# Two blocks on one core: a modelled DMA queue in the order planner, four key projections side by side, and the last three gate projections in token halves

## The chip, the cores and the metric

One core of one Trainium2 chip runs the whole program as one launch. The metric is the device time of that core in microseconds; lower is better. 2911.86 us is the median of three runs of the kernel before (2909.01 to 2912.65).

## The reference, cut to what matters

512 tokens of width 2048 go through two residual blocks. What follows is the frame that the change touches: the memory projections at the start, and the gate and the final norm at the end.

```python
def memory_cross_attention(xq, mem_n, w_kv, qn_g, kn_g):       # first block
    q = rms_norm(xq.reshape(B, S, XA_HEADS, XA_DIM), qn_g)
    kv = jnp.einsum("bmd,de->bme", mem_n, w_kv)                # 256 memory rows
    k = rms_norm(kv[..., :XA_WIDTH]..., kn_g); v = kv[..., XA_WIDTH:]...
    p = jax.nn.softmax(q . k * XA_DIM ** -0.5)
    return p . v

def first_block(x, mem, ...):
    mem_n = rms_norm(mem, mem_norm_g)
    h = rms_norm(x, norm_g)
    proj = jnp.einsum("bsd,de->bse", h, dn_w_in)
    mix = deltanet_branch(proj[..., :DN_MIX_COLS], ...)        # conv, gated delta rule
    xa = memory_cross_attention(xq, mem_n, ...)
    y = jnp.concatenate([mix, xa], axis=-1) * jax.nn.silu(z)
    return x + jnp.einsum("bse,ed->bsd", y, w_out)

def second_block(x, p, ...):
    ...                                                        # mLSTM and HGRN2 mixers
    h = h + jnp.einsum('bsc,cd->bsd', y, w_out)
    e = jnp.einsum('bsr,rd->bsd', p, w_pe)
    gate = jax.nn.sigmoid(jnp.einsum('bsd,de->bse', rmsnorm(h, pe_norm_w), w_pg))
    h = h + gate * e
    return rmsnorm(h, final_norm_w)
```

## The kernel before, in words

Activations lie feature-major: a tile is 128 features by 512 tokens (256 for the memory), and 2048 features are 16 such tiles. Every large product is done in float32 by a split: ScalarE rounds an operand to `hi` (L120), VectorE makes the rest `lo` (L131), and TensorE adds hi times hi, hi times lo and lo times hi into one PSUM bank (L167). A weight job is 128 output features; its weights come in four pieces of 4 feature tiles, 128 by 512 numbers or 256 KB each. A piece goes through a `raw` buffer (six of them), a `hi` buffer and a `lo` buffer (five each), and feeds 12 products on TensorE: for each of the four feature tiles hi times the high and the low half of the activation, then lo times the high half.

The program is written by a planner in Python, `Driver` (from L80). It keeps an estimated clock for each engine (`clk`), and a generator for every piece of work. `run` (L348) takes the ready task of the best priority, or else the next three products, and issues its instructions on the engines' queues at once. So the clocks only set the order; the chip runs each engine's queue strictly in that order, and every instruction waits for what it needs. Loads stand on SyncE's queue in order too. In the planner of before a weight piece was held to be there at 3 us behind TensorE's clock, or at 4.5 us plus 1.5 us for each piece, whichever is later (L274), and any other load after 2.3 us (L171).

The stages that matter here:

- **Start.** SyncE loads a piece of `w_k` and a tile pair of the memory (`mraw`, L450) in turn, eight times, and then a piece and a tile of x (`xraw`, L456) in turn, sixteen times. Of the 16 jobs of the memory (8 keys, 8 values, 256 columns in every product) the first two stand side by side: a pair of feature tiles feeds both before the next is needed (L1739, `add`). `mem_task` (L560) scales and splits the memory (`mh`, `ml`) and then sums its squares (`mraw`); `evac_k` and `evac_v` wait for the sum. `x_task` (L591) squares x on ScalarE (`xsq`), sums on VectorE (`xsum`), gets the reciprocal norm over TensorE (`ss`), and then `part` scales each of the 16 tiles of x and splits it (`xraw`, `xh`, `xl`).
- **Query projections.** The first jobs on x (`acc<-xh`) use these 16 tiles one by one.
- **Middle.** The first block's convolutions and delta rule, output, the second block's mixers, and its output.
- **End.** Jobs `je[i]` and `jg[i]` alternate (16 of each). `evac_g` (L1689) scales the gate's product, takes the sigmoid, multiplies by `e`, adds to `h` and adds the square to a sum. The last gate job is done in two halves of 256 tokens. At the end of each half comes the sum over features (`ss`), the reciprocal root (ScalarE Ln and Exp), and 16 products of 128 by 256 (`out`), 13 of them on VectorE and 3 on GpSimd, which leave as 8 stores of 256 KB.

## Time and profile before

| what | value |
|---|---|
| median of three runs | 2911.86 us (2909.01 to 2912.65) |
| the profiled execution, its own time | 2909.73 us |
| its span in the trace | 2907.8 us |
| TensorE busy | 2852.8 us, 98% |
| VectorE busy | 1713.4 us, 59% |
| ScalarE busy | 1389.0 us, 48% |
| GpSimd busy | 80.7 us, 3% |
| DMA | 308.92 MB, mean 106 GB/s |

TensorE is busy nearly all the time, so a look at shares tells little; what is left to gain lies where TensorE waits. Matmul durations overlap in the trace: the distance between two starts is what a product costs. "Idle before, releaser" names what ended a wait.

### The profile page before, as it was taken

What the parts mean: (1) busy time and instruction counts of PE and PEld (TensorE: products, weight loads), DVE (VectorE), ACT (ScalarE), POOL (GpSimd) and SP (SyncE); (2) the same over time, 40 slices, a digit from 0 to 9 for tenths busy, and PEclk for the clock granted to TensorE, in tenths of its full rate; (3) what the DMA queues carried; (4) which work ended last, traced back from release to release, by engine and by line L of the source; (5) the groups of instructions that cost most, each with busy time, mean ns of one, the idle gap of its engine ahead of it and who ended that gap; (6) DMA issues with size and microseconds to landing.
All of it is one profiled execution on the core that took longest, in us unless ns stands there. A gap on an engine that the chain in (4) does not pass through costs nothing. (4 is left out here: it accounts for less than half of the span.)

```text
span 2907.8 us, 40891 instructions
## 1 busy us (share of the span) xinstructions
PE 2852.8 (98%) x14936; PEld 2382.5 (82%) x14936; DVE 1713.4 (59%) x3285; ACT 1389.0 (48%) x2627; POOL 80.7 (3%) x178
## 2 busy tenths in 40 slices
PE   7999999999999999999999999999999999999997
PEld 7877887788788888888888878888888888888886
DVE  6746677778777777635333464455655556444445
ACT  6544645565545555435222334444554556433433
POOL 0000000100000100000000000000000000000000
PEclk9999999999999999999999999999999999999998
DMA  7422422233222332354433433222222222333233
GB/s 244 145 80 93 122 94 88 95 98 98 83 89 98 95 98 91 102 169 127 130 119 119 151 104 109 91 77 80 84 84 77 91 84 88 116 122 110 95 98 109
DMA packets 177865, 308.92 MB, mean 106 GB/s; under 512 B 25216, under 2 KB 32000, under 8 KB 177664
## 3 DMA queue, kind: packets, MB, share of 16 engines
q1 hardware_dynamic: 177664, 306.31, 33.1%
q8 instruction: 117, 1.92, 0.3%
q14 instruction: 84, 0.69, 0.1%
HBM read 290.24 MB, written 15.99 MB: 105 GB/s over the span
## 5 line engine op out<-in xcount | busy, mean ns | idle before, releaser
L131 DVE TENSOR_TENSOR lo<-raw,hi 128x512 fp32r<-128x512 f32 x948 | 638.5, 685 | 624.4 <-ACT hi L120 605.5
L120 ACT ACTIVATE hi<-raw 128x512 fp32r<-128x512 f32 x956 | 586.9, 621 | 868.6 <-PE acc L167 762.4
L167 PE MATMUL acc<-xh,hi 128*128 128x512 f32 x1424 | 582.5, 409 | 0.7 <-ACT xh L120 0.4
L167 PE MATMUL acc<-xl,hi 128*128 128x512 f32 x1424 | 556.2, 391 | 2.8 <-DVE xl L131 2.7
L167 PE MATMUL acc<-xh,lo 128*128 128x512 f32 x1408 | 551.4, 392 | 4.5 <-DVE lo L131 4.4
L167 PE MATMUL acc<-x2h,hi 128*128 128x512 f32 x1040 | 415.8, 400 | 0.0
L167 PE MATMUL acc<-x2l,hi 128*128 128x512 f32 x1040 | 405.2, 390 | 0.0
L167 PE MATMUL acc<-x2h,lo 128*128 128x512 f32 x1024 | 399.8, 390 | 0.0
L167 PEld LDWEIGHTS acc<-xh,lo 128*128 128x128 f32 x1408 | 264.4, 188 | 63.8 <-DVE lo L131 6.2
L167 PEld LDWEIGHTS acc<-xl,hi 128*128 128x128 f32 x1424 | 268.4, 189 | 54.6 <-DVE xl L131 4.0
L167 PEld LDWEIGHTS acc<-xh,hi 128*128 128x128 f32 x1424 | 268.2, 188 | 53.6 <-issue 1.7
L167 PE MATMUL acc<-ph,hi 128*128 128x512 f32 x768 | 298.8, 389 | 0.0
L167 PE MATMUL acc<-pl,hi 128*128 128x512 f32 x768 | 298.8, 389 | 0.0
L167 PE MATMUL acc<-ph,lo 128*128 128x512 f32 x768 | 298.8, 389 | 0.0
L167 PEld LDWEIGHTS acc<-x2h,lo 128*128 128x128 f32 x1024 | 192.2, 188 | 41.5
L167 PEld LDWEIGHTS acc<-x2l,hi 128*128 128x128 f32 x1040 | 195.7, 188 | 37.0
L167 PEld LDWEIGHTS acc<-x2h,hi 128*128 128x128 f32 x1040 | 195.6, 188 | 37.2
L167 PEld LDWEIGHTS acc<-pl,hi 128*128 128x128 f32 x768 | 144.1, 188 | 30.1
L167 PEld LDWEIGHTS acc<-ph,lo 128*128 128x128 f32 x768 | 144.1, 188 | 29.9
L167 PEld LDWEIGHTS acc<-ph,hi 128*128 128x128 f32 x768 | 144.1, 188 | 29.8
L134 DVE SCALAR_TENSOR_TENSOR cv<-acc,c_dn_conv,cv 128x511 f32<-128x511 f32 x144 | 107.3, 747 | 35.6 <-ACT cv L120 32.1
L131 DVE TENSOR_TENSOR Xb<-Xb,Nb 128x16 f32<-128x16 f32 (+30 forms) x372 | 113.7, 306 | 8.8
(321 smaller groups left out, 3631.4 us busy)
## 6 DMA issues: line engine op xcount, KB each, us to landing
raw<-w_qkv SPq DMA_DIRECT2D x192, 256.0 KB, 3.1
raw<-w_out SPq DMA_DIRECT2D x192, 256.0 KB, 2.9
raw<-w_z SPq DMA_DIRECT2D x128, 256.0 KB, 3.2
raw<-w_pg SPq DMA_DIRECT2D x68, 256.0 KB, 3.0
gR<-dgc SPq DMA_DIRECT2D x48, 256.0 KB, 3.9
raw<-w_k SPq DMA_DIRECT2D x32, 256.0 KB, 4.8
raw<-w_v SPq DMA_DIRECT2D x32, 256.0 KB, 3.7
raw<-w_xq SPq DMA_DIRECT2D x32, 256.0 KB, 3.1
```

Source lines behind the costliest of these rows:

```text
L120: self.nc.scalar.activation(out=out, in_=in_, func=func, **kw)
L131: self._v(eng, free_size(out)).tensor_tensor(out=out, in0=a, in1=b, op=op)
L134: self._v(None, free_size(out)).scalar_tensor_tensor(out=out, in0=a, scalar=s, in1=b, op0=op0, op1=op1)
L167: self.nc.tensor.matmul(out, lhsT=lhsT, rhs=rhs, start=start, stop=stop, is_transpose=True if tr else None)
```

## The change

The planner gets a clock for SyncE and one for the DMA queue (`land`, in place of the fixed delays): a load starts when SyncE can issue it, the queue then takes 1.1 us for 256 KB at first and 0.7 us later, and the load is held to be there a little after. Weight pieces, the first loads and all later loads and stores through `dma` use it. Since every clock steers the order, instructions move in the whole program, though the same work is done.

At the start the first four key jobs stand side by side instead of two; the eight tile pairs of the memory are loaded over the first 13 pieces of weights, with six tiles of x between them, and the other ten tiles of x after 16 pieces. The squares of x are summed on GpSimd instead of VectorE.

At the end the last three gate jobs instead of one are done in token halves, all three of the first half ahead of the second half's. Their squares move from ScalarE to VectorE. The 16 output products of a half are a task of their own (`out_half`); four of the 16 are on GpSimd.

```diff
 
     def __init__(self, tc, wp, psp, sp):
         self.tc, self.nc, self.wp, self.psp, self.sp = tc, tc.nc, wp, psp, sp
-        self.clk = dict(pe=0.0, act=0.0, dve=0.0, pool=0.0)
+        self.clk = dict(pe=0.0, act=0.0, dve=0.0, pool=0.0, sp=1.2)
+        self.dq = 0.0
         self.tau = 0.0
         self.tasks = []
         self.units = []
@@ -168,9 +169,17 @@
                               is_transpose=True if tr else None)
         self._on("pe", c, LP)
 
-    def dma(self, out, in_, lat=2.3):
+    def land(self, n=128 * T, extra=0.1):
+
+        t = max(self.clk["pe"], self.clk["sp"])
+        self.clk["sp"] = t + 0.5
+        self.dq = max(self.dq, t + 2.0)
+        self.dq += (0.7 if self.dq > 9 else 1.1) * n / (128 * T)
+        return self.dq + 0.25 + extra
+
+    def dma(self, out, in_, extra=0.9, n=128 * T):
         self.nc.sync.dma_start(out=out, in_=in_)
-        self.tau = max(self.tau, self.clk["pe"]) + lat
+        self.tau = max(self.tau, self.land(n, extra))
 
 
     def slot(self, shape=(128, T), dt=F32, name="s", reserve=0):
@@ -271,7 +280,7 @@
             j, c0, n = self.pieces[self.i_dma]
             raw = self.wp.tile([128, KC, 128], F32, tag="raw", bufs=RAW, name="raw")
             self.nc.sync.dma_start(out=raw[:, :n, :j.w.shape[2]], in_=j.w[:, c0:c0 + n])
-            self.pieces[self.i_dma] = (j, c0, n, raw, max(self.clk["pe"] + 3.0, 4.5 + 1.5 * self.i_dma))
+            self.pieces[self.i_dma] = (j, c0, n, raw, self.land(n * 128 * j.w.shape[2]))
             self.i_dma += 1
             if self.i_dma <= self.nhead:
                 self.head(self.i_dma)
...
@@ -444,19 +453,31 @@
     for k in range(KT):
         xraw.append(d.slot_now(name="xraw"))
 
+    loads = [[] for _ in range(1 + 3 * KT)]
+    for i in range(len(mraw)):
+        loads[4 * (i // 2) + (i % 2 if i < 2 else i % 2 - 1)].append(("m", i))
+    n = 0
+    for i in range(len(loads)):
+        if n < KT and (i % 4 in (1, 2) and i > 4 if i < KT else i >= KT):
+            loads[i].append(("x", n))
+            n += 1
+
     def first_loads(i):
 
-        if i < len(mraw):
-            nc.sync.dma_start(out=mraw[i], in_=A["memT"][:, 2 * i:2 * i + 2])
-        elif i < len(mraw) + KT:
-            k = i - len(mraw)
+        for what, k in loads[i] if i < len(loads) else ():
+            if what == "m":
+                nc.sync.dma_start(out=mraw[k], in_=A["memT"][:, 2 * k:2 * k + 2])
+                f_m[k].tau = d.land()
+                f_m[k].done = True
+                continue
             if k == 0:
                 nc.sync.dma_start(out=ident, in_=A["ident"])
                 nc.sync.dma_start(out=norm_g, in_=A["norm_g"])
             nc.sync.dma_start(out=xraw[k], in_=A["xT"][:, k])
-            d.give(f_x[k])
-            f_x[k].tau = d.clk["pe"] + 3.0
-
+            f_x[k].tau = d.land(extra=0.5)
+            f_x[k].done = True
+
+    f_m = [Fut() for _ in mraw]
     f_x = [Fut() for _ in range(KT)]
     resetb = const.tile([128, T], F32, name="resetb")
     nc.vector.memset(resetb, 1.0)
...
@@ -560,7 +581,8 @@
     def mem_task():
         hs = []
         for i, t in enumerate(mraw):
-            d.tau = 3.8 + 1.5 * i
+            d.tau = 0.0
+            yield from need(f_m[i])
             yield
             tau = d.tau
             hi = yield from slot(dt=F32R, name="mh")
@@ -577,6 +599,7 @@
         t0 = d.tau
         for i, t in enumerate(mraw):
             d.tau = t0
+            yield from need(f_m[i])
             yield from d.calm(AHEAD)
             t = t.rearrange("p k m -> p (k m)")
             act(t, t, AF.Square)
@@ -592,13 +615,14 @@
         ssum = yield from slot(name="xsum")
         for k, t in enumerate(xraw):
             yield from need(f_x[k])
+            yield
             yield from d.calm(AHEAD)
             q = yield from slot(name="xsq")
             act(q, t, AF.Square)
             if k == 0:
-                cp(ssum, q)
+                cp(ssum, q, eng=pool)
             else:
-                tt(ssum, ssum, q, ADD)
+                tt(ssum, ssum, q, ADD, eng=pool)
             free(q)
         f = Fut()
         yield from ones_sum([ssum], T, 1.0 / D, f)
...
@@ -1686,13 +1710,18 @@
             give(f_pe[i], e)
         return gen
 
+    NSP = 3
+
+    def on_pool(k):
+        return k % 3 == 1 and k < KT - NSP
+
     def evac_g(i):
         def gen(job):
             r = yield from need(f_r2)
             w = cst("fin_w")
             c, n = job.cols, job.n
-            t = yield from slot(name="gt")
-            t = t[:, :n]
+            job.t = yield from slot(name="gt")
+            t = job.t[:, :n]
             tt(t, job.ps, r[:, c], MUL)
             d.acc_done()
             act(t, t, AF.Sigmoid)
@@ -1702,44 +1731,60 @@
             tt(t, t, e[:, c], MUL)
             h = f_h2[i].val[:, c]
             tt(h, h, t, ADD)
-            if i < KT - 1:
-                free(t, e)
+            if c.stop == T:
+                free(e)
+            if i < KT - NSP:
+                free(job.t)
                 yield from sum_sq("h3", h, i == 0)
-                if i % 4 == 3:
+                if on_pool(i):
                     act(h, h, AF.Copy, scale=w[:, i:i + 1])
                 return
-            act(t, h, AF.Square)
+            tt(t, h, h, MUL)
+            if i < KT - 1:
+                tt(ssq["h3"][:, c], ssq["h3"][:, c], t, ADD)
+                free(job.t)
+                return
             yield
             ss = yield from bank("ss")
             mm(ss[:, :n], ones, ssq["h3"][:, c], start=True, stop=False)
             mm(ss[:, :n], ones, t, start=False, stop=True)
             rstd(ss[:, :n], t, 1.0 / D)
             d.free_bank()
-            t0 = d.tau
-            for k0 in range(0, KT, 2):
+            last = c.stop == T
+            d.spawn(out_half(c, n, t, last), 4 if last else 30)
+        return gen
+
+    def out_half(c, n, t, last):
+
+        w = cst("fin_w")
+        t0 = d.tau
+        for k0 in range(0, KT, 2):
+            o = yield from slot((128, 2, n), name="out")
+            te = []
+            for k in (k0, k0 + 1):
                 d.tau = t0
-                o = yield from slot((128, 2, n), name="out")
-                for k in (k0, k0 + 1):
-                    d.tau = t0
-                    yield
-                    h = f_h2[k].val[:, c]
-                    if k % 4 == 3 and k < KT - 1:
-                        tt(o[:, k - k0], h, t, MUL, eng=pool)
-                    else:
-                        stt(o[:, k - k0], h, w[:, k:k + 1], t, MUL, MUL)
-                nc.sync.dma_start(out=out[:, k0:k0 + 2, c], in_=o)
-        return gen
+                if not last:
+                    yield from d.calm(AHEAD)
+                h = f_h2[k].val[:, c]
+                if on_pool(k):
+                    tt(o[:, k - k0], h, t, MUL, eng=pool)
+                else:
+                    stt(o[:, k - k0], h, w[:, k:k + 1], t, MUL, MUL)
+                te.append(d.tau)
+            d.tau = max(te)
+            yield
+            nc.sync.dma_start(out=out[:, k0:k0 + 2, c], in_=o)
 
 
     first_loads(0)
     d.head = first_loads
-    d.nhead = len(mraw) + KT
+    d.nhead = len(loads) - 1
...
     d.spawn(mem_task(), 1)
     d.spawn(x_task(), 2)
     jk = [Job(A["w_k"][e], M, evac_k(e), NM) for e in range(2 * XH)]
     jv = [Job(A["w_v"][e], M, evac_v(e), NM) for e in range(2 * XH)]
-    d.add(jk[0], jk[1])
-    for j in jk[2:] + jv[:-2]:
+    d.add(*jk[:4])
+    for j in jk[4:] + jv[:-2]:
         d.add(j)
     jv[-1].drop = True
     d.add(jv[-2], jv[-1])
@@ -1857,12 +1902,14 @@
     d.add(je[0])
     d.add(je[1])
     d.add(jg[0], jg[1])
-    for i in range(2, KT - 1):
+    for i in range(2, KT - NSP):
         d.add(je[i])
         d.add(jg[i])
-    d.add(je[KT - 1])
-    d.add(Job(A["w_pg"][KT - 1], X3, evac_g(KT - 1), n=T // 2))
-    d.add(Job(A["w_pg"][KT - 1], X3, evac_g(KT - 1), n=T // 2, prio=4, c0=T // 2))
+    for i in range(KT - NSP, KT):
+        d.add(je[i])
+    for c0 in (0, T // 2):
+        for i in range(KT - NSP, KT):
+            d.add(Job(A["w_pg"][i], X3, evac_g(i), n=T // 2, c0=c0, prio=4))
     with tc.manual_schedule():
         d.run()
```

Left out of the diff are the calls of `dma` in the gates' and mixers' tasks, which now give the size of what they load.

Three places in the queues, before and after. The first is ScalarE's queue at the start (`hi<-raw`: a weight piece's high half; `mh`: the memory's; `xsq`: squares of x; `mraw`: squares of the memory). Before:

```order
L120 ACTIVATE hi<-raw 128x512
L120 ACTIVATE mh<-mraw,c_mem_norm_g 128x256 x2
L120 ACTIVATE hi<-raw 128x512
L120 ACTIVATE mh<-mraw,c_mem_norm_g 128x256 x2
L120 ACTIVATE xsq<-xraw 128x512
L120 ACTIVATE hi<-raw 128x512
L120 ACTIVATE mh<-mraw,c_mem_norm_g 128x256 x2
L120 ACTIVATE hi<-raw 128x512
L120 ACTIVATE xsq<-xraw 128x512
```

After:

```order
L121 ACTIVATE hi<-raw 128x512
L121 ACTIVATE mh<-mraw,c_mem_norm_g 128x256 x2
L121 ACTIVATE hi<-raw 128x512
L121 ACTIVATE xsq<-xraw 128x512
L121 ACTIVATE hi<-raw 128x512 x2
L121 ACTIVATE mh<-mraw,c_mem_norm_g 128x256 x2
L121 ACTIVATE xsq<-xraw 128x512
L121 ACTIVATE hi<-raw 128x512
L121 ACTIVATE mh<-mraw,c_mem_norm_g 128x256 x2
```

Both begin with the fourth weight piece, and in both the first square of x stands behind the fifth. On SyncE's queue, which is not shown, the first tile of x is loaded behind the eighth weight piece before and behind the fifth after.

The second place is VectorE's queue where x is scaled and split, from the row in which the sum of squares goes to TensorE (`ql<-xsum`) or near it (`lo<-raw`: a weight piece's low half; `vt`: a value job's result; `xraw<-xraw`: scaling a tile of x; `xl`: its low half). Before, the last part of that stretch:

```order
L131 TENSOR_TENSOR xl<-xraw,xh 128x512
L131 TENSOR_TENSOR lo<-raw,hi 128x512
L131 TENSOR_TENSOR xl<-xraw,xh 128x512
L134 SCALAR_TENSOR_TENSOR xraw<-xraw,norm_g,xsum 128x512 x3
L131 TENSOR_TENSOR lo<-raw,hi 128x512
L134 SCALAR_TENSOR_TENSOR xraw<-xraw,norm_g,xsum 128x512 x2
L131 TENSOR_TENSOR xl<-xraw,xh 128x512 x3
L134 SCALAR_TENSOR_TENSOR xraw<-xraw,norm_g,xsum 128x512
L131 TENSOR_TENSOR xl<-xraw,xh 128x512 x2
L134 SCALAR_TENSOR_TENSOR xraw<-xraw,norm_g,xsum 128x512
L131 TENSOR_TENSOR lo<-raw,hi 128x512
L131 TENSOR_TENSOR xl<-xraw,xh 128x512 x2
```

After, the same part:

```order
L132 TENSOR_TENSOR lo<-raw,hi 128x512
L135 SCALAR_TENSOR_TENSOR xraw<-xraw,norm_g,xsum 128x512 x4
L132 TENSOR_TENSOR xl<-xraw,xh 128x512
L135 SCALAR_TENSOR_TENSOR xraw<-xraw,norm_g,xsum 128x512
L132 TENSOR_TENSOR xl<-xraw,xh 128x512 x5
L135 SCALAR_TENSOR_TENSOR xraw<-xraw,norm_g,xsum 128x512 x2
L132 TENSOR_TENSOR lo<-raw,hi 128x512
L135 SCALAR_TENSOR_TENSOR xraw<-xraw,norm_g,xsum 128x512 x3
L132 TENSOR_TENSOR xl<-xraw,xh 128x512 x2
L135 SCALAR_TENSOR_TENSOR xraw<-xraw,norm_g,xsum 128x512
L132 TENSOR_TENSOR xl<-xraw,xh 128x512 x3
L132 TENSOR_TENSOR lo<-raw,hi 128x512
```

The `lo` of the 70th weight piece stands in front of the block of after; the first row is that piece. Behind it 11 scalings and 12 low halves are left (one low half follows the last row). Before, behind the 70th piece's `lo`, which is the row between the first two `xl`, 7 scalings and 8 low halves are left. On TensorE's queue the sum of squares (`ss`) stands behind 600 of the 768 products of the memory before, and behind 684 of them after.

The third place is the end of VectorE's queue (`gt`, `h1r`, `ssum`: the evacuation of a gate job). Before:

```order
L131 TENSOR_TENSOR lo<-raw,hi 128x512 x4
L131 TENSOR_TENSOR gt<-acc,ssum 128x256
L131 TENSOR_TENSOR gt<-gt,e 128x256
L131 TENSOR_TENSOR h1r<-h1r,gt 128x256
L131 TENSOR_TENSOR gt<-acc,ssum 128x256
L131 TENSOR_TENSOR gt<-gt,e 128x256
L131 TENSOR_TENSOR h1r<-h1r,gt 128x256
L134 SCALAR_TENSOR_TENSOR out<-h1r,c_fin_w,gt 128x256 x26
```

After, from the evacuation of the last job but one:

```order
L132 TENSOR_TENSOR gt<-acc,ssum 128x256
L132 TENSOR_TENSOR gt<-gt,e 128x256
L132 TENSOR_TENSOR h1r<-h1r,gt 128x256
L132 TENSOR_TENSOR gt<-h1r 128x256
L132 TENSOR_TENSOR ssum<-ssum,gt 128x256
L132 TENSOR_TENSOR lo<-raw,hi 128x512 x3
L135 SCALAR_TENSOR_TENSOR out<-h1r,c_fin_w,gt 128x256 x10
L132 TENSOR_TENSOR gt<-acc,ssum 128x256
L132 TENSOR_TENSOR gt<-gt,e 128x256
L132 TENSOR_TENSOR h1r<-h1r,gt 128x256
L132 TENSOR_TENSOR gt<-h1r 128x256
L135 SCALAR_TENSOR_TENSOR out<-h1r,c_fin_w,gt 128x256 x14
```

Ten output products of the first half now stand ahead of the last job's evacuation, and three `lo` of the last job's own weights stand behind the evacuation of the job before it.

## Rows read from the trace of the kernel before

**Rows 1.** The page: TensorE's busy time, share of the span, instructions.

```profile
PE 2852.8 (98%) x14936; PEld 2382.5 (82%) x14936; DVE 1713.4 (59%) x3285; ACT 1389.0 (48%) x2627; POOL 80.7 (3%) x178
```

**Rows 2.** Busy time by stretch (us from the span's start: length, then busy time and instructions of each engine, granted clock of TensorE, DMA share, GB/s).

```profile
0.00:72.70 72.70, 58.02 (x437) 56.30 (x438) 49.61 (x98) 48.69 (x97) 0.20 (x4) 0.98 0.76 244
...
10.00:20.00 10.00, 6.62 (x49) 6.28 (x48) 5.75 (x13) 5.83 (x13) 0.00 (x0) 1.00 0.97 313
...
2880.00:2907.80 27.80, 8.10 (x59) 7.19 (x58) 16.94 (x35) 7.59 (x14) 5.33 (x6) 0.72 0.45 151
```

**Rows 3.** What TensorE waited for, over the whole span (us in total, times, longest).

```profile
PE acc L167 <- DVE lo L131: 9.2, 6, 3.2
...
PE pst L167 <- DVE ud L131: 3.2, 1, 3.2
PE tr L167 <- DVE pr L131: 3.0, 4, 1.3
...
PE p L167 <- DVE XA L141: 2.5, 2, 1.3
PE num L167 <- DVE Cs L134: 2.1, 1, 2.1
```

**Rows 4.** The same from the start to 135 us.

```profile
PE acc L167 <- ACT mh L120: 6.3, 1, 6.3
PE acc L167 <- DVE lo L131: 4.7, 3, 2.7
PE acc L167 <- ACT hi L120: 3.4, 1, 3.4
PE acc L167 <- DVE xl L131: 2.7, 2, 1.8
```

**Rows 5.** ScalarE in order of time, 13 to 20 us (start, duration, instruction, idle time before it and its releaser).

```profile
13.30 0.61 ACT L120 ACTIVATE hi<-raw 128x512 fp32r<-128x512 f32 x1
13.82 0.90 ACT L120 ACTIVATE mh<-mraw,c_mem_norm_g 128x256 fp32r<-128x256 f32 x2
18.39 0.63 ACT L120 ACTIVATE xsq<-xraw 128x512 f32<-128x512 f32 x1 [3.68 <-DMA xraw<-xT]
18.93 0.61 ACT L120 ACTIVATE hi<-raw 128x512 fp32r<-128x512 f32 x1
```

**Rows 6.** The two stretches ahead of the end in which TensorE's granted clock was at half (columns as in Rows 2).

```profile
21.37:24.78 3.41, 3.41 (x19) 3.41 (x18) 3.23 (x7) 3.41 (x8) 0.00 (x0) 0.50 1.03 371
...
553.85:557.26 3.41, 3.41 (x55) 2.48 (x54) 3.18 (x11) 1.38 (x4) 0.00 (x0) 0.50 0.82 254
```

**Rows 7.** TensorE in order of time: two early products, the sum of squares of the third and fourth key job's head, that of x, the first product of the query projections, and the last two of the first query job.

```profile
7.82 0.41 PE L167 MATMUL acc<-ml,hi 128*128 128x256 f32 x1
8.04 0.41 PE L167 MATMUL acc<-mh,lo 128*128 128x256 f32 x1
...
62.70 0.28 PE L167 MATMUL acc<-mh,lo 128*128 128x256 f32 x1
62.82 0.28 PE L167 MATMUL ss<-qh,ones_r 128*128 128x256 f32 x1
...
94.15 0.39 PE L167 MATMUL ss<-qh,ones_r 128*128 128x512 f32 x1
...
115.38 0.40 PE L167 MATMUL acc<-xh,hi 128*128 128x512 f32 x1
...
130.68 0.40 PE L167 MATMUL acc<-xl,hi 128*128 128x512 f32 x1
130.91 0.39 PE L167 MATMUL acc<-xh,lo 128*128 128x512 f32 x1
```

**Rows 8.** VectorE in order of time, 120 to 131 us.

```profile
120.28 2.07 DVE L134 SCALAR_TENSOR_TENSOR xraw<-xraw,norm_g,xsum 128x512 f32<-128x512 f32 x3
...
124.20 1.89 DVE L131 TENSOR_TENSOR xl<-xraw,xh 128x512 fp32r<-128x512 f32 x3
...
129.14 1.28 DVE L131 TENSOR_TENSOR xl<-xraw,xh 128x512 fp32r<-128x512 f32 x2
```

**Rows 9.** The end in order of time, from one answer for each engine: TensorE, VectorE, ScalarE, GpSimd, SyncE.

```profile
2885.95 0.59 PE L167 MATMUL ss<-ssum,ones 128*128 128x256 f32 x2
...
2888.89 0.70 PE L167 MATMUL ss<-gt,ones 128*128 128x256 f32 x2 [1.49 <-ACT gt L120]
...
2886.14 0.42 DVE L131 TENSOR_TENSOR gt<-acc,ssum 128x256 f32<-128x256 f32 x1 [3.15 <-PE acc L167]
2887.05 0.42 DVE L131 TENSOR_TENSOR gt<-gt,e 128x256 f32<-128x256 f32 x1 [0.48 <-ACT gt L120]
2887.51 0.43 DVE L131 TENSOR_TENSOR h1r<-h1r,gt 128x256 f32<-128x256 f32 x1
2889.59 13.19 DVE L134 SCALAR_TENSOR_TENSOR out<-h1r,c_fin_w,gt 128x256 f32<-128x256 f32 x26 [1.65 <-ACT gt L120]
...
2890.04 0.42 ACT L120 ACTIVATE gt<-gt 128x256 f32<-128x256 f32 x1
...
2889.64 5.33 POOL L131 TENSOR_TENSOR out<-h1r,gt 128x256 f32<-128x256 f32 x6 [399.46 <-PE ss L167]
...
2890.97 12.77 SPq L1730 DMA_DIRECT2D outT<-out  x16
```

**Rows 10.** VectorE's output products by stretch (busy time and count, GpSimd's beside them): while GpSimd is at its own, and behind that.

```profile
2890.86:2895.18 4.32, 4.32 (x6) 4.11 (x5) 0.63 0.53 177
2895.18:2902.77 7.59, 7.59 (x20) 0.00 (x0) 0.50 0.95 315
```

More of the change, by code (lines that the diff above doesn't have):

```diff
@@ L761, in evac_ab @@
         yield
-        d.dma(dgc, rows[0:32])
+        d.dma(dgc, rows[0:32], n=32 * T)
         pt = yield from transpose4(rows)
@@ L1299, in evac_if @@
         for j, r in enumerate((mu, wi, en)):
-            d.dma(drow[j], r[0:32], lat=0)
-        d.dma(dws, ws[:, 0:NCH])
+            d.dma(drow[j], r[0:32], n=32 * T)
+        d.dma(dws, ws[:, 0:NCH], n=32 * NCH)
         t0 = d.tau
@@ L1309, in evac_if @@
         yield
-        d.dma(wsb, bc(dws, 0, 128))
+        d.dma(wsb, bc(dws, 0, 128), n=32 * T)
         free(w, fx, nb, mu, wi, en, rows, sp_)
@@ L1347, in ml_task @@
             yield
-            d.dma(t, mlg["drow"][j, h:h + 1].broadcast_to((128, T)))
+            d.dma(t, mlg["drow"][j, h:h + 1].broadcast_to((128, T)), 1.5)
             rr.append(t)
```

## The prediction

> **What bounds the kernel now.** I read the page first: TensorE is busy for 98% of the span [rows 1]. What an edit of order can win is therefore time in which TensorE waits, and time behind its last product. The stretches [rows 2] put most of that at the two ends: 58.0 of the first 72.7 us are busy, and 8.1 of the last 27.8. The waits say who is late. At the start [rows 4] the first product waits 6.3 us for the first piece and memory tile; then 3.4 us are lost behind a `hi` and 4.7 us behind `lo`; where the query projections begin, 2.7 us behind `xl`. In the middle [rows 3] the waits that I can name add up to 9.2 - 4.7 + 3.2 + 3.0 + 2.5 + 2.1 = 15.3 us, none of them on a load.
>
> Behind a stall the clock can fall. The 3.4 us wait lies at 16 to 20 us, and in the 3.41 us from 21.37 on the granted clock is 0.5, the 1.2 GHz level; behind a 3.2 us wait near 549 us it is so again [rows 6]. One such stretch costs up to half of its length, 1.7 us.
>
> The cause of the 3.4 us is plain in ScalarE's rows [rows 5]: the sixth `hi` was queued behind a square of x, and that waited 3.68 us for its load. The planner believed in a load that had not come.
>
> **Start, what goes.** Compare at one place: the `ss` at 62.82 us [rows 7] stands behind 348 products of the memory. A warm product of 256 columns costs 0.12 us (62.70 to 62.82), a cold one 0.21 (7.82 to 8.04). Undisturbed that `ss` would start at 6.3 + 348 x 0.12 + 23 cold ones x 0.09 + 3 earlier pairs of `ss` at 0.25 = 50.9 us. So 11.9 us are lost: 4.7 + 3.4 in waits, 1.7 to the clock, 2.1 in small gaps. The first product stays at 6.3 us: its piece and its memory tile are still loaded first.
>
> **Start, what comes.** Four jobs side by side use a pair of memory tiles for four pieces, so the loads per piece fall, and the DMA's 313 GB/s [rows 2] (0.84 us for 256 KB) has to bring 38 tiles, 32 us, by the 20th piece, which TensorE reaches at about 36 us; the loads are just in time and ScalarE's queue follows their order. What I expect to stay: `lo` of the fourth and eighth piece stand behind memory splits on VectorE, 0.7 and 0.9 us late; the key jobs' chain of squares on ScalarE and VectorE in turn, three heads back to back, with the next `lo` behind it, some 2.5 us (before, its like cost 2.7 [rows 4]).
>
> The sums of squares go to GpSimd. When both engines work on two-input products of 256 columns, one of VectorE's starts every 4.32 / 5 = 0.87 us where GpSimd runs, and every (7.59 - 0.47) / 18 = 0.395 us where it does not [rows 10]: each of GpSimd's costs VectorE 0.47 us, so an add of 512 columns, not in this trace, some 0.94 us, between 0 (VectorE idle) and 1.8 (GpSimd's own duration of 0.89 us [rows 9], doubled). VectorE's own add costs 0.60. Of the sixteen, the first four or five fall where VectorE is paced with TensorE; I take 1.0 us of delay there, the others meet slack. The Trainium skill ("SBUF — State Buffer", Who interferes with whom) says that a VectorE instruction with two SBUF inputs and a GpSimd instruction that reads SBUF lock each other out for a whole instruction. The trace agrees, with 0.87 against 0.395 us. By that rule moving 16 adds takes 16 x 0.60 = 9.6 us off VectorE's queue and gives back up to 16 x 0.94 = 15.0 us; were all of that late for TensorE, the start would win nothing.
>
> Lost after: 0.7 + 0.9 + 2.5 + 1.0 = 5.1 us, so 6.8 less than before; of the small gaps I let half stay. The memory's products should end **5.8 us earlier** (bounds 2, when loads are late once more, and 9.8 = 4.7 + 3.4 + 1.7, when nothing is).
>
> **Where that goes: the first query job.** x can be scaled only when its norm is known. On TensorE's queue that sum stands behind 600 of 768 products before and 684 after. Before, 21.2 us pass from it to the first query product (94.15 to 115.38 [rows 7]); after, 84 x 0.12 and a transposition, 10.4 us. VectorE then owes 16 scalings at 0.66 us ((2.07 - 0.75) / 2) and 16 low halves at 0.60 ((1.89 - 0.69) / 2) [rows 8], 20.2 us, with `lo` pieces between. Before, it was dense only from 119 to 130.4 us, and the last `xl` ended the job: its last product is at 130.91, 15.7 us behind the first query product's place at 115.38 (10.9 us of products and 4.8 of waiting).
>
> After, VectorE's queue has the 70th `lo` ahead of 11 scalings and 12 low halves. That `lo` needs a `hi` buffer which TensorE gives back when it has done the first query piece, 12 x 0.23 = 2.7 us behind the start; with the `hi` and the `lo` itself 4.2 us. Then 11 x 0.66 + 12 x 0.60 + two `lo` = 15.7 us, and 0.7 for the last products: 20.6 us where it was 15.7. So **4.9 us are given back**, and TensorE should wait for `xl` for about 9.5 us in place of 2.7, over 4 us of it in one piece. Of the start's 5.8 us, 0.9 stay (bounds -3 and +5).
>
> **End.** Let J be the end of the last gate job that is whole in both kernels. Before: three `e` jobs (3 x 1.36), two whole gate jobs (48 x 0.227 = 10.9 each) and two halves (48 x 0.12 = 5.76): the last product ends 37.3 us behind J, at 2885.95, and the span 21.85 us later [rows 9]: J + 59.2. Those 21.85 are 3.6 to the first output product, 13.2 for 26 of them, 5.0 to the end.
>
> After: six halves, so J + 38.6 and 0.9 for the first half's `ss`, 1.3 + 0.9 more than before on TensorE. The first half's `ss` stands 54 products into the second half, its norm is there 10 us before the end. But VectorE's queue decides. Let H be the first half's end, J + 21.4. The second job of the second half ends at H + 12.4. Its evacuation is six steps in turn with ScalarE at 0.46 (2886.14 to 2886.60 and on): to H + 15.2. Behind it stand three `lo` of the last job, 1.8 us: TensorE comes to the first of them at H + 14.1 and must wait about 1.8 us. Then ten output products, 10 x 0.395, to H + 20.95; only then the last job's evacuation, though its product ended at H + 19.9. Five steps 2.3, `ss` 0.7, Ln and Exp 0.85: H + 24.8. The two leftover products of the first half hide in that. Twelve on VectorE, four of them against GpSimd's: 4 x 0.87 + 8 x 0.395 = 6.6; to the end 4.3 to 5.0, since the queue of stores is shorter (8 instead of 16). Sum H + 35.7 to 36.4, J + 57.1 to 57.8: a **gain of 1.8 us** (bounds 0, and 4.6 without the ten products and the three `lo` in the way). The 8 pieces more to split are 8 x 0.60 on VectorE and as much on ScalarE; they hide beside products, but for the three.
>
> **Middle.** The same instructions in another order. Its 15.3 us of waits and the 1.7 us of half clock [rows 3, 6] come from chains between VectorE and ScalarE, which the new clock does not touch; none was on a load. I take no change, with bounds of 6 us each way (a third of them gone or as many more).
>
> **The sum.** 0.9 + 1.8 + 0 = 2.7 us. The profiled execution took 2909.7 us, 2.2 less than the median, so 2907.0 against its own time and 2909.2 against the median: I say **2909**. Its own range is 2904 to 2914.
>
> **Rivals.**
>
> *The covers hold.* If VectorE is not late at the query job (the norm earlier, the scalings between the last value pieces) and the last evacuation is not behind the ten products, the start keeps 5.8 to 8 and the end 4.6: 2911.9 - 10.4 to 12.6 = 2899.3 to 2901.5. For it: VectorE is 59% busy and was idle for much of 40 to 60 us. Against it: a queue is strictly in order.
>
> *Slower: a broken chain in the delta rule.* Between 300 and 1200 us ScalarE does a batch of conv activations with two table loads ahead of the recurrence's `u`, and TensorE stood 3.2 us on it (`pst` [rows 3]). A new order can put more of the twelve groups so. Each is 3.2 us, and 4.9 when the clock falls behind it. With the 2.7 us gained it is slower by over 0.2% from (5.8 + 2.7) / 4.1, the mean of the two, two or three more such places; with three, 2911.9 - 2.7 + 12.3 = 2921, with two 2917.
>
> *The new clock is no better.* It takes 0.7 us for 256 KB, the rows say 0.84. If ScalarE again waits on a square of x ahead of a `hi`, the start loses 3.4 + 1.7 again and the first query job still gives back 4.9: 2909.2 + 5.1 = 2914.3, within 0.2%.
>
> **How the numbers follow.** The forecast has 0.47, the covers 0.27, the broken chain 0.12, the clock 0.14. About 0.2%, 5.8 us, is what a measurement of this kernel can tell from no change. Faster by more: the 0.27 and 0.06 of the forecast's edge, 0.33. Slower: 0.12 and 0.02 of the last case, 0.14. Between: 0.53. For eight in ten the range must reach into the covers and to the slower side's edge: 2899.5 to 2917.
>
> **What would show it.** Right: the first `ss` behind 348 products at 55 to 59 us; no wait of ScalarE on x of over 1 us ahead of 30 us; TensorE's wait on `xl` up from 2.7 to 8 us or more; in the end a wait of 1 to 2 us on a `lo`, ten outputs ahead of the last evacuation, and 17 us or less from the last product to the end. Wrong: a wait on `xl` under 4 us, or the middle's waits away from 15 us by more than 6.

## The result, and the profile after

The changed kernel takes 2930.15 us (median of four runs, 2927.0 to 2931.75) beside 2911.77 us for the kernel before on the same chip: a ratio of 1.0058, 95% interval 1.0045 to 1.0071. It is slower, by 18 us, and outside the predicted range of 2899.5 to 2917. The profiled execution took 2929.07 us, span 2927.3 us, 19.5 us more than the span of before. Two of the eleven executions of a run below, e4_tail, the profiled one among them, took about twice as long as the others; its ratio leaves them out, and its trace is not used.

Busy shares say nothing of it, again. The page, to be set beside [rows 1]:

```profile
PE 2866.4 (98%) x15032; PEld 2394.3 (82%) x15032; DVE 1719.6 (59%) x3289; ACT 1401.1 (48%) x2640; POOL 99.7 (3%) x196
```

What finds the place of the loss is to take the same product in both traces (products stand in the same order inside a stage) and to subtract its start times:

| the same product | before, us | after, us | after minus before |
|---|---|---|---|
| first of the query projections | 115.38 | 112.63 | -2.75 |
| the 178th on x | 164.52 | 167.02 | +2.50 |
| last on x | 1337.62 | 1339.84 | +2.22 |
| 97th of the first block's output | 1359.61 | 1382.08 | +22.47 |
| first of the second block | 1686.01 | 1708.47 | +22.46 |
| last on its input (x2) | 2514.66 | 2535.31 | +20.65 |
| last of the 13th gate job | 2848.37 | 2869.02 | +20.65 |
| end of the span | 2907.8 | 2927.3 | +19.5 |

So 2.5 us are lost by the 178th product on x, the second block gives 1.8 back and the end 1.15, and 20.25 us go within some 40 us at the first output projection (`w_out`). There the kernel before waited for nothing, 96 products in 21.76 us:

```profile
1337.62 0.39 PE L167 MATMUL acc<-xh,lo 128*128 128x512 f32 x1
1337.85 0.39 PE L167 MATMUL acc<-ph,hi 128*128 128x512 f32 x1
...
1359.61 0.39 PE L167 MATMUL acc<-ph,hi 128*128 128x512 f32 x1
```

The stretches of after (columns as in [rows 2]):

```profile
0.00:72.70 72.70, 60.69 (x460) 58.39 (x461) 49.60 (x96) 50.09 (x99) 9.06 (x11) 1.00 0.77 251
10.00:20.00 10.00, 10.00 (x74) 10.00 (x74) 5.92 (x12) 7.46 (x15) 2.15 (x2) 1.00 0.93 275
118.90:125.70 6.80, 5.64 (x13) 4.36 (x14) 6.36 (x11) 2.68 (x5) 0.00 (x0) 0.50 0.02 5
558.00:566.00 8.00, 6.44 (x69) 4.57 (x68) 5.20 (x17) 4.91 (x12) 0.00 (x0) 0.79 0.20 64
1341.00:1365.00 24.00, 10.85 (x33) 7.87 (x34) 11.16 (x25) 10.04 (x20) 0.00 (x0) 0.72 0.47 160
1347.70:1361.35 13.65, 5.31 (x13) 4.15 (x14) 6.54 (x18) 4.06 (x9) 0.00 (x0) 0.50 0.40 139
2907.60:2911.00 3.40, 3.40 (x18) 3.40 (x17) 3.40 (x9) 0.00 (x0) 0.00 (x0) 0.50 0.50 165
```

From 1341 on TensorE works 10.85 of 24 us, and for 13.65 us the granted clock is at half (0.50), the 1.2 GHz level. The waits over the whole span (us, times, longest), beside [rows 3]:

```profile
PE acc L168 <- DVE pl L132: 13.5, 8, 11.7
PE acc L168 <- DVE lo L132: 7.0, 7, 2.0
PE acc L168 <- ACT mh L121: 6.9, 1, 6.9
PE acc L168 <- DVE xl L132: 4.3, 3, 2.4
PE pst L168 <- DVE ud L132: 3.8, 2, 3.1
...
PE ss L168 <- ACT qh L121: 2.0, 2, 1.7
PE ss L168 <- DVE gt L132: 1.9, 1, 1.9
PE acc L168 <- ACT ph L121: 1.5, 1, 1.5
...
PE acc L168 <- ACT xh L121: 1.2, 1, 1.2
```

The first line is new: `pl` is the low half of the first block's result y, the moving operand of `w_out`. Three queues at that place tell the rest. SyncE, issues in order of time, first before, then after (`y`: reload of y; `raw`: a weight piece; `lm`: masks for the second block):

```profile
1304.27 0.38 SPq L172 DMA_DIRECT2D y<-yscr  x1
1306.57 0.33 SPq L273 DMA_DIRECT2D raw<-w_z  x1
1306.95 0.43 SPq L172 DMA_DIRECT2D y<-yscr  x1
```

```profile
1330.92 0.42 SPq L181 DMA_DIRECT2D y<-yscr  x1
1333.26 3.05 SPq L282 DMA_DIRECT2D raw<-w_out  x2
1336.40 0.38 SPq L181 DMA_DIRECT2D y<-yscr  x1
1338.70 3.04 SPq L282 DMA_DIRECT2D raw<-w_out  x2
1341.84 3.71 SPq L181 DMA_DIRECT2D y<-yscr  x8
1345.59 0.65 SPq L181 DMA_DIRECT2D xr<-xT  x1
1346.28 2.71 SPq L1479 DMA_DIRECT2D lm<-lmask  x2
```

Before, one y load goes with every weight piece (2.72 us), and the last is issued at 1306.95, 31 us ahead of the first `w_out` product. After, one goes with every second piece, and at 1341.84, when TensorE is at its first `w_out` product, eight are left. The two orders differ because `y_loader` is one sequential generator: it issues a load, sets its clock to the landing, and only then issues the next. The old planner gave a load 2.3 us, less than a piece; the new `land` comes to 3.85 us here (2 + 0.7 + 0.25 + 0.9), more than a piece. The splits of y (`ph`, `pl`) wait for the loader's end (`f_all`).

VectorE in order of time, after:

```profile
1341.91 1.28 DVE L132 TENSOR_TENSOR pl<-y,ph 128x512 fp32r<-128x512 f32 x2
1353.31 0.63 DVE L1480 CAST lmask<-lm 128x512 uint8<-128x512 f32 x2 [10.11 <-DMA lm<-lmask]
...
1355.30 2.49 DVE L132 TENSOR_TENSOR pl<-y,ph 128x512 fp32r<-128x512 f32 x4
```

Two `pl` are made, then the in-order queue has the cast of the masks, whose load stands behind the eight y loads, and VectorE waits 10.11 us for it with `pl` work ready behind. ScalarE stands still as well: behind four `ph` its queue has an exponential of the same task (`lbv`), which waits 9.72 us for VectorE. Before, the same cast stood behind 26 of the 32 `pl` and waited 2.10 us that TensorE did not feel:

```profile
1342.06 0.63 DVE L1456 CAST lmask<-lm 128x512 uint8<-128x512 f32 x2 [2.10 <-DMA lm<-lmask]
```

TensorE after, in order of time:

```profile
101.89 0.39 PE L168 MATMUL ss<-qh,ones_r 128*128 128x512 f32 x1
...
112.63 0.40 PE L168 MATMUL acc<-xh,hi 128*128 128x512 f32 x1
...
117.14 0.49 PE L168 MATMUL acc<-xh,hi 128*128 128x512 f32 x1 [1.16 <-ACT xh L121]
120.06 0.80 PE L168 MATMUL acc<-xl,hi 128*128 128x512 f32 x1 [2.42 <-DVE xl L132]
...
1339.84 0.39 PE L168 MATMUL acc<-xh,lo 128*128 128x512 f32 x1
1341.72 0.50 PE L168 MATMUL acc<-ph,hi 128*128 128x512 f32 x1 [1.50 <-ACT ph L121]
...
1356.04 0.80 PE L168 MATMUL acc<-pl,hi 128*128 128x512 f32 x1 [11.73 <-DVE pl L132]
1356.64 0.63 PE L168 MATMUL acc<-ph,lo 128*128 128x512 f32 x1
...
1382.08 0.39 PE L168 MATMUL acc<-ph,hi 128*128 128x512 f32 x1
...
2906.78 0.39 PE L168 MATMUL acc<-x3h,lo 128*128 128x256 f32 x1 [1.98 <-DVE lo L132]
```

The 20.25 us are 13.5 + 1.5 of waits; half of the 5.31 us in which TensorE worked at the 1.2 GHz level behind the long wait, 2.7; and the remaining 2.6 in the slow first products behind nine waits and in pauses too short to be listed.

### The profile page after: what moved, and what is told of

Read it like the earlier page. It is cut to its first block, busy times and chain, and to the rows that moved or that the text cites. A ratio compares the mean times of both kernels' runs of the same rounds, so it can differ in the third digit from the quotient of the medians.

```text
span 2927.3 us, 41145 instructions
## 1 busy us (share of the span) xinstructions
PE 2866.4 (98%) x15032; PEld 2394.3 (82%) x15032; DVE 1719.6 (59%) x3289; ACT 1401.1 (48%) x2640; POOL 99.7 (3%) x196
## 5 line engine op out<-in xcount | busy, mean ns | idle before, releaser
L132 DVE TENSOR_TENSOR lo<-raw,hi 128x512 fp32r<-128x512 f32 (+1 forms) x956 | 648.2, 690 | 624.4 <-ACT hi L121 589.0
L121 ACT ACTIVATE hi<-raw 128x512 fp32r<-128x512 f32 (+1 forms) x964 | 592.0, 621 | 871.2 <-PE acc L168 759.3
L168 PE MATMUL acc<-pl,hi 128*128 128x512 f32 x768 | 300.7, 392 | 13.5 <-DVE pl L132 13.5
```

What stands on the lines that cost most here:

```text
L121: self.nc.scalar.activation(out=out, in_=in_, func=func, **kw)
L132: self._v(eng, free_size(out)).tensor_tensor(out=out, in0=a, in1=b, op=op)
L168: self.nc.tensor.matmul(out, lhsT=lhsT, rhs=rhs, start=start, stop=stop, is_transpose=True if tr else None)
```

## The experiments

The loader theory: the slower pace of the y loads, with the masks' load behind them, is the loss. Rivals: the new order loses a little everywhere; or only one link of the chain (late splits, the masks, late loads) matters. Each ratio is to the kernel before on the same chip; edits are to the changed kernel unless said.

| run | median, us | ratio to before | 95% interval |
|---|---|---|---|
| e1_pace | 2911.45 | 0.9992 | 0.9983 to 1.0001 |
| e2_slow | 2929.74 | 1.0056 | 1.0040 to 1.0071 |
| e3_lm | 2915.09 | 1.0007 | 0.9997 to 1.0016 |
| e4_tail | 2913.14 | 0.9995 | 0.9985 to 1.0004 |
| e5_norm | 2908.85 | 0.9984 | 0.9975 to 0.9993 |
| e6_both | 2907.53 | 0.9978 | 0.9968 to 0.9987 |
| e7_dvesum | 2905.35 | 0.9973 | 0.9963 to 0.9983 |
| e8_notail | 2912.07 | 0.9993 | 0.9984 to 1.0002 |
| e9_normdve | 2901.46 | 0.9961 | 0.9946 to 0.9975 |
| e10_best | 2902.36 | 0.9962 | 0.9948 to 0.9976 |

**e1_pace.** The y loader alone at its old pace:

```diff
+            t0 = max(d.tau, d.clk["pe"])
             d.dma(t, yscr[i])
+            d.tau = t0 + 2.3
```

> The changed kernel, with one thing put back: the loader of the first block's y tiles (y_loader) hands its clock on after 2.3 us, as before, in place of the modelled landing; the new clock stays everywhere else. The loader theory (one y load per two weight pieces, so that the last eight are issued when TensorE already needs the split tiles) expects 2909 to 2912 us, about 18 to 21 less than the changed kernel's 2930, no wait of VectorE on lm of over 3 us, splits ph and pl under way 20 us or more before the first w_out product, and no half-clock stretch at 1345 to 1365. The theory that the middle was re-ordered at large by the new clock (many small losses) expects it to stay at 2925 or more, since all other loads keep the new clock.

It came to 0.9992, 0.66% (19 us) under the changed kernel's 1.0058. TensorE's waits between 1335 and 1385 us are

```profile
PE acc L168 <- DVE pl L132: 0.4, 2, 0.2
```

and the clock stays whole there. The loader theory holds; "a little everywhere" falls. One point was missed: the splits start 13 us ahead of the first `w_out` product (1321.8 and 1334.87), not 20 or more, and 11 `pl` stand ahead of the cast, where it was 26 before and 2 after.

**e2_slow.** The kernel before, with only that loader slowed:

```diff
-            d.dma(t, yscr[i])
+            d.dma(t, yscr[i], lat=4.6)
```

> The kernel before, with one thing changed: y_loader's loads are held to take 4.6 us in place of 2.3, which makes one y load per two weight pieces, and leaves five of them to the end. Nothing of the change is in it. The loader theory expects 2924 to 2932 us (12 to 20 more than before): VectorE with two pl ahead of the cast of lmask, a wait of 6 to 10 us there on the load of lm, TensorE waiting as long for pl, and the clock at half behind that. The theory of re-ordering at large expects no more than 3 us of difference.

One number in the old kernel makes a loss of the same size, 1.0056 beside 1.0058; in the traces 17.0 us of it lie between the last product on x and the 97th of `w_out`. VectorE in order of time:

```profile
1341.94 1.29 DVE L131 TENSOR_TENSOR pl<-y,ph 128x512 fp32r<-128x512 f32 x2
1349.93 0.65 DVE L1456 CAST lmask<-lm 128x512 uint8<-128x512 f32 x2 [6.70 <-DMA lm<-lmask]
```

Five y loads were left instead of eight, so the wait is 6.70 us and TensorE's on `pl` 10.2.

**e3_lm.** The loads stay late; the masks' task begins two jobs later:

```diff
-    d.spawn(after(f_ob[0], gate0(), d), 40)
+    d.spawn(after(f_ob[2], gate0(), d), 40)
```

> The changed kernel, with the task of the masks (hg_consts, which loads and casts lmask) begun with the third w_out job in place of the first. The y loads stay late. If the wait that cost the time is VectorE's in-order wait on lm, ahead of the split of tiles that are already there, it falls to 2910 to 2916 us: of 13.5 us of waits on pl 2 to 4 stay, and no 13 us at half clock. If late splits alone are the cost, whatever stands in VectorE's queue, it stays at 2925 to 2931. If late y loads are the cost by their own landing (eight loads one behind the other), TensorE's waits move to ph and pl of the last y tiles, with 6 us or more: 2918 to 2924.

1.0007: 0.51% (15 us) of the loss gone, with the y loads and the splits as late as in the changed kernel. VectorE now makes six `pl` at once, and TensorE's waits there are

```profile
PE acc L168 <- DVE pl L132: 1.9, 8, 0.4
PE acc L168 <- ACT ph L121: 1.5, 1, 1.5
```

So VectorE's wait on the masks was most of the loss: some 15 of the 19 us by the medians. By single traces it is 12.5 of 18.2: from the last product on x to the 97th of `w_out` it is 42.2 us in the changed kernel, 29.7 in e3_lm, 24.1 in e1_pace (22.0 before). The other 4 to 6 us go with splits that are just in time (3.4 us of waits against e1_pace's 0.4, and 3.4 us at half clock from 1343.3 on); no run tests that share by itself. Late loads by themselves were expected to show as 6 us or more on the last y; they don't.

**e4_tail and e8_notail.** The changed end alone on the kernel before, and e1_pace without it; the edit is the change's diff from `NSP` on, and its jobs:

```diff
-    for i in range(2, KT - 1):
+    for i in range(2, KT - NSP):
...
+    for c0 in (0, T // 2):
+        for i in range(KT - NSP, KT):
+            d.add(Job(A["w_pg"][i], X3, evac_g(i), n=T // 2, c0=c0, prio=4))
```

> The kernel before, with the change's end alone: the last three gate jobs in token halves, squares on VectorE, four outputs on GpSimd and the task out_half; no new clock, no new start. The prediction's end term expects 1.8 us less than before (bounds 0 and 4.6); the changed kernel's trace, set against the end of the last whole gate job, shows 1.2 us less with a half-clock stretch of 3.4 us in it: 2909.5 to 2911 for a before of 2911.8. A rival, that the halves' eight pieces more and the evacuations in between slow the jobs ahead, expects 1 us or more slower.

> e1_pace with the end of the kernel before (only the last gate job in halves). Up to the last whole job that both have, the two traces should agree. The prediction's end term expects this kernel 1.8 us slower than e1_pace; the traces of the changed kernel and of e1_pace, each set against the end of the 13th gate job, show 1.1 us. If the end as changed is worth nothing, the two are within 0.5 us.

The times can't tell the end from nothing: 0.9995 alone, 0.9993 without it against e1_pace's 0.9992. The traces of four other kernels can: from the last product of the 13th gate job to the end of the span it is 59.4 us in the kernel before (2848.37 to 2907.8) and 59.2 in e8_notail (2852.50 to 2911.7), against 58.3 in the changed kernel (2869.02 to 2927.3) and in e1_pace (2846.20 to 2904.5). A gain of about 1 us.

**e5_norm.** On e1_pace, the squares of x no longer wait for the modelled adds:

```diff
         for k, t in enumerate(xraw):
+            d.tau = 0.0
             yield from need(f_x[k])
```

> e1_pace, and in the planner's task for x the square of the next tile no longer waits for GpSimd's modelled add of the one before. By the order, the sum of squares of x then stands on TensorE's queue behind 492 memory products in place of 684, and behind the 70th lo VectorE owes 3 scalings and 3 low halves in place of 11 and 12. The theory that the first query job pays for the late norm (the prediction's step, sized 4.9 us) expects the waits on xl and xh there to fall from 6.2 us to under 1 and the clock to stay up at 118 to 126 us: 5 to 7 us less than e1_pace, a ratio to the kernel before of about 0.997. The rival, that VectorE cannot do the 32 operations between the value pieces without making lo late, expects new waits on lo before 112 us of as much, and no gain.

Half of each theory. The waits on `xl` and `xh` are gone, but TensorE waits 3.4 us for a `vt` and 1.1 for a `lo` at 60 to 140 us instead, and the gain on e1_pace, 0.08%, is within the intervals. The first query product comes 7.9 us later (120.55 against 112.64 us), and the way from it to the 178th product on x is 9.1 us shorter (44.8 against 53.9). GpSimd and VectorE at that place:

```profile
62.63 10.31 POOL L132 TENSOR_TENSOR xsum<-xsum,xsq 128x512 f32<-128x512 f32 x7 [20.16 <-ACT xsq L121]
```

```profile
70.04 6.37 DVE L132 TENSOR_TENSOR lo<-raw,hi 128x512 fp32r<-128x512 f32 x5
76.33 2.89 DVE L135 SCALAR_TENSOR_TENSOR xk<-xk,c_xa_kg,sq 128x256 f32<-128x256 f32 x2
```

Seven adds now run back to back, and five `lo` take 6.37 us, 1.27 each, where 0.60 is usual back to back.

**e7_dvesum.** On e1_pace, the sum back on VectorE:

```diff
-                cp(ssum, q, eng=pool)
+                cp(ssum, q)
...
-                tt(ssum, ssum, q, ADD, eng=pool)
+                tt(ssum, ssum, q, ADD)
```

> e1_pace, with the sum of x's squares back on VectorE (the 16 operations that the change gave to GpSimd). By the order, the sum then stands behind 618 memory products in place of 684 and VectorE owes 7 scalings and 9 low halves behind the 70th lo in place of 11 and 12. The prediction took 1.0 us of delay at the start for what GpSimd's adds cost VectorE; with that the start is 1 us earlier here, and the first query job's waits shrink by some 4 x 0.66 + 3 x 0.60 = 4.4 us at most: 2 to 5 us less than e1_pace. The rival, that moving the adds off VectorE was worth it (16 x 0.60 us of its queue), expects more waits on lo before 60 us and a time equal to e1_pace or 1 to 3 us more.

0.9973, 0.19% (5.5 us) under e1_pace. The first query product starts where it did (112.69 against 112.64 us), so the start itself is no earlier; the 178th product on x is 4.3 us earlier (162.25 against 166.50). The gain goes with the norm: x's sum stands at 93.59 us in place of 101.90.

**e6_both, e10_best, e9_normdve.** The end with `lo` ahead of the evacuation, on e5_norm and on e7_dvesum; e9_normdve has e5_norm's line too:

```diff
             act(t, t, AF.Sigmoid)
+            if KT - NSP <= i < KT - 1:
+                yield
...
-                    yield from d.calm(AHEAD)
+                    yield from d.calm(3.0)
```

> e5_norm, and at the end the evacuation of the first jobs in halves pauses behind its sigmoid, so that the lo of the last weight pieces can be issued ahead of it, and the first half's outputs may run further ahead of TensorE. In e1_pace's trace TensorE waited 2.0 us on such a lo and ran 3.4 us at half clock behind it; 2.0 + 1.7 + two outputs fewer behind the last evacuation (0.9) = 4.6 us at most. Expected against e5_norm: 2 to 4.6 us less, no wait on lo of over 0.5 us behind the last whole job. A rival, that the outputs put ahead now delay the evacuations in turn, expects 0 to 1 us of gain or a loss.

> e7_dvesum with the end of e6_both: y loads at the old pace, x's sum on VectorE, the last lo ahead of the evacuation. e7_dvesum came to 0.9973 of the kernel before; in the traces the end of e6_both, from the 13th gate job on, is 56.7 us long against 58.3 in e7_dvesum. Expected 0.9968 (some 2904 for a before of 2913), 1 to 2 us less than e7_dvesum; if the outputs put ahead only move the delay from TensorE's lo to the last evacuation, it is equal to e7_dvesum.

> e10_best with the square of x's next tile no longer held behind the modelled add of the one before (the edit of e5_norm, here with the adds on VectorE). By the order the sum of squares of x stands behind 573 memory products, between e7_dvesum's 618 and e5_norm's 492, and VectorE owes 6 scalings and 6 low halves behind the 70th lo (7 and 9 in e7_dvesum). If an earlier norm goes on helping, the first query job loses 1 us less than in e7_dvesum (3.7 us of waits there): 1 us less than e10_best. If VectorE's queue is the limit either way, as in e5_norm, where a vt of the values came 3.4 us late, it is 1 to 3 us slower than e10_best, with waits on vt or lo at 70 to 112 us.

The `lo` wait at the end is gone in each, and a wait on `gt` and `ssum` grows instead (in e10_best 2.3 and 0.9 us, in e7_dvesum `lo` 2.0 and `gt` 1.9): 0.06% (less than 2 us) in e6_both, where 2 to 4.6 us were expected, and 0.11% in e10_best, both inside the intervals. The line of e5_norm does no harm once the adds are VectorE's: no wait on `vt` in e9_normdve, and on `xl` 2.0 us in place of e10_best's 2.7. The two end level, at 0.9961 and 0.9962: some 10 to 11 us faster than the kernel before.

## Why the prediction was wrong

**The step that failed is "Middle"**, in these words: "chains between VectorE and ScalarE, which the new clock does not touch; none was on a load". That no wait of before was on a load is true, and proved the wrong thing: the loads were covered, and the clock that spaced them was what the change replaced. The lookahead of `y_loader` hung on 2.3 us being less than the 2.72 us of a piece. I had named `dma` as changed and did not ask which generators take its time into their own; the order after shows the eight y loads in one row. What stood in its place is 20.25 us at `w_out`. The prediction's own sign of being wrong came in: the middle's waits that it named were 10.5 us in place of 15.3, and `w_out` added 15.0. The rival "a broken chain" had the right sign and the wrong place: the result is 21 us above the forecast, five of its places at 4.1 us each, but `pst` waited 3.8 us in all, 0.6 more than [rows 3].

Outside of `w_out` the middle stayed inside its bounds (+2.50 to +2.22 up to 1340 us, and -1.8 behind), but that the first part came out level was luck. In the trace of after the granted clock is at half for 3.4 us at 562.6, 883.5 and 1033.7 us; before, that is so once, at 553.9 [rows 6]. From the 178th product on x to the last it is 1173.1 us before, 1172.8 after, and 1168.1 in e1_pace, which has no such stretch: the new order gains some 3 us there, which the half clock took back.

**Start.** "5.8 us earlier" came to 2.75, inside its bounds of 2 and 9.8. The named losses were right: 2.8 us of waits on `lo` and 2.0 on the key chain (`qh`), against 0.7 + 0.9 + 2.5 + 1.0. The wait on `hi` of [rows 4] is gone (10.00 of 10 us busy from 10 to 20), and ScalarE's longest wait on x ahead of 30 us was 0.95. Missing were 0.6 at the first product (a wait of 6.9 us against 6.3) and the small gaps, which came to some 4 us in place of 2.1 and did not halve. What follows the 348th memory product starts at 60.28 us, not at 55 to 59; busy to 72.70 us is 60.69 against 58.02 [rows 2].

**The first query job.** "4.9 us are given back" measured 5.25 (-2.75 to +2.50). The form was off: `xl` 4.3 us, not 8 or more, with 1.2 on `xh` and 6.8 us at half clock. x's sum stands at 101.89 us, 7.7 behind its place in [rows 7]. That this is the cause, e7_dvesum and e5_norm show together: the sum earlier, by adds on either engine, takes the loss away (from the first query product to the 178th on x it is 49.1 us before, 54.4 after, 49.6 and 44.8 in these two).

**GpSimd's adds.** The 1.0 us taken for the start was not found there (e7_dvesum). The changed kernel, VectorE and then GpSimd:

```profile
87.82 0.69 DVE L132 TENSOR_TENSOR lo<-raw,hi 128x512 fp32r<-128x512 f32 x1 [0.30 <-ACT hi L121]
...
89.25 1.04 DVE L132 TENSOR_TENSOR lo<-raw,hi 128x512 fp32r<-128x512 f32 x1
...
92.35 1.07 DVE L132 TENSOR_TENSOR lo<-raw,hi 128x512 fp32r<-128x512 f32 x1 [0.71 <-ACT hi L121]
```

```profile
88.45 1.30 POOL L132 TENSOR_TENSOR xsum<-xsum,xsq 128x512 f32<-128x512 f32 x1 [1.49 <-ACT xsq L121]
91.57 1.29 POOL L132 TENSOR_TENSOR xsum<-xsum,xsq 128x512 f32<-128x512 f32 x1 [1.82 <-ACT xsq L121]
```

A `lo` beside an add takes 1.04 or 1.07 us instead of 0.69, and ends 0.54 or 0.56 us behind the add's end (89.75, 92.86). The Trainium skill ("SBUF — State Buffer", Who interferes with whom) says that a VectorE instruction with two SBUF inputs and a GpSimd instruction that reads SBUF contend for a shared port pair, under an exclusive lock. The trace agrees, and gives the price: beside a single add the `lo` pays for what is left of it; back to back, as in e5_norm, it pays 0.67 each time. What the move to GpSimd cost most was not the lock, though, but the later norm.

**End.** "Gain of 1.8" measured 1.15, from the 13th gate job on. The wait on `lo` was 1.98 us for the predicted 1.8, ten outputs stood ahead of the last evacuation, and the twelve behind it took 6.80 us for 6.6. But VectorE waited 0.75 us for that last product, so the ten delayed nothing; TensorE had been held by the `lo` and by 3.4 us at half clock behind it (0.50 from 2907.6 to 2911.0), which the sum did not have.

## What to carry to other kernels

A latency in an order planner is also a pace wherever a generator issues one load after the other's landing: compare it with the period of what it runs beside, and look ahead by count, not by time (the second is advice that no run here tried). When a clock model changes, list every loop that takes its time from it, and read the new order at each place where a stage first uses loaded data. And an operation that waits for a load belongs behind the ready work in an in-order queue: the cast of a mask that is first used 620 us later (1976 us) cost 12 to 15 us.

## What was not expected of the hardware

The better clock was nearer the truth: in the changed kernel the y loads up to 1300 us landed this long after their issue,

```profile
DMA to landing us min/median/max: 3.4/3.5/4.4
```

so 2.3 us was too short by a third and made the faster kernel.

The clock does not fall at the same waits every time. The changed kernel and e1_pace have TensorE's products in the same order up to 1234 us. At 558 to 566 us both wait for the same `P` (1.35 and 1.36 us), and the granted clock is 0.79 after and, in e1_pace,

```profile
558.00:566.00 8.00, 6.42 (x83) 4.88 (x82) 5.25 (x16) 5.07 (x11) 0.00 (x0) 1.00 0.21 63
```

There and at two later places the changed kernel's trace falls behind e1_pace's by 1.4, 1.5 and 1.6 us, about half of a 3.4 us stretch each, in the same instructions. Two traces of one order differ by 4.6 us for this alone, so a gain of a few us does not show in the spans of two traces.
